# Layer 1 of a hybrid decoder step: keys in the index queries' room, stacked values later in the sample workspace's room, sample search behind the prompt's scores

## The chip, the core and the metric

The kernel runs on one core of one Trainium2 chip. The metric is the device time of one execution in microseconds (us), median of several executions. TensorE (PE) multiplies matrices and transposes, VectorE (DVE), ScalarE (ACT) and GpSimd (POOL) work element by element, and SyncE (SP) and ACT issue most of the transfers. Each engine works through its own list of instructions in order.

## The reference, cut to what matters

One inference step of a two-layer decoder, with a prompt of 1024 tokens and eight sample rows (one new token each, 1024 cached). The change lies in layer 1, whose mixer is a sparse attention: an indexer scores every key for every query, the best 256 keys of each query are kept, and 16 query heads attend to those alone over 4 key/value heads.

```
def dsa_attend(qpos, q, qi, wi, k, v, ki, topk):
    dots = jnp.einsum('bqhd,bkd->bqhk', qi, ki).astype(jnp.float32)
    score = jnp.einsum('bqhk,bqh->bqk', jax.nn.relu(dots), wi.astype(jnp.float32))
    causal = kpos[None, None, :] <= qpos[None, :, None]
    _, idx = lax.top_k(jnp.where(causal, score, -jnp.inf), topk)
    k_sel = gather(k, idx)
    v_sel = gather(v, idx)
    s = jnp.einsum('bqngd,bqknd->bqngk', qg, k_sel).astype(jnp.float32) * (HEAD_DIM ** -0.5)
    p = jax.nn.softmax(jnp.where(valid, s, -jnp.inf), axis=-1).astype(v.dtype)
    o = jnp.einsum('bqngk,bqknd->bqngd', p, v_sel)
...
def dsa_mixer(xn, pos, past_kv, past_idx_k, page_table, w_in, idx_g, idx_b, w_out):
    q, k, v, qi, ki, wi = split_cols(xn @ w_in, C_SIZES)
    if page_table is None:
        o = map_query_blocks(lambda pb, qb, qib, wib: dsa_attend(pb, qb, qib, wib, k, v, ki, topk), pos, q, qi, wi)
    else:
        o = dsa_attend(pos, q, qi, wi, k_all, v_all, ki_all, topk)
    return o @ w_out, (jnp.stack([k, v], axis=2), ki)
```

## The kernel before, in words

Layer 1's mixer takes about the stretch from 1340 to 2000 us of the span. Its parts run side by side:

- **The projection** (dense_cols, L339 to L341 by way of mm3): for each tile of 128 output columns (index queries qi, queries q 0 to 7, keys k 0 and 1, values v 0 and 1, in this order) three chunks of tokens with 24 matmuls each, d<-xh and d<-xl. The weight of each tile is split into a high and a low part (whif on ACT, wlof on DVE). ev_raw copies a finished tile to "raw1", and post_q, post_k or post_v goes on: rotation (rope, a shuffle on DVE and three products on POOL), splits into high and low, and natural-order copies by TensorE transposes (nat_out, "b<-small,raw").
- **Index scores** (idx_scores, L1956 on PE, L229 `sc<-rl` on DVE), for six blocks of 128 queries in groups [2,3], [4,5] and [6,7]; blocks 0 and 1 need no choice.
- **The prompt's search** (top_select): bit by bit, 31 steps for each group, a count of scores above a threshold (L1993 on DVE `tjk<-sc` or `tjk<-top`, or L215 `tjk<-sc` on ACT) and three small operations on 128x2 tiles. It ends in the mask of each block (flags l1.m2 to l1.m7).
- **The sample's search** (gen_dsa_dec): index scores of the cache, then eight steps, each a count over 128x1025 on DVE (L2263 `tjk<-hk`), a matmul with 128x1 output that sums over partitions (L2268 `b<-small,grpc`), and small operations; then ranks (two scans), eight transposes (L251 `b<-small,hk`), one-hot rows (L218 `hk<-tmpd`), and eight matmuls that turn them into a list of rows (L2324 `b<-hk`, "the list" below), which DVE reads (`tmpd<-b`). Later come the gathers of the listed rows and the sample's attention.
- **The prompt's attention** (dsa_units): for each of eight query blocks and four key/value heads a unit of four heads. A score group of TensorE (L530 `s<-ks,q1b`), a masked maximum on DVE (L533), an exponential on ACT, transposes, and the product with the values: blocks 0 to 4 (PLAIN) take the natural values "nat" kept in VF (L2099), blocks 5 to 7 take "stacked" values vs, a high and a low copy side by side (L2103). The queries q1b come by transfers from device memory. The out projection starts when all 32 units and the sample's attention are done.

Four large tiles of one pool matter here, each of the pool's size: hx (index queries of the prompt), hk (the sample's workspace), ks1 (the keys' stacks) and vs1 (the values' stacks); the last two can only be made in room that hx and hk have left.

The order of the program comes from two stages. Generators (streams) yield costs and wait for flags ("need"); a driver lets the one with the least accumulated cost go on. Its list then goes through a scheduler that places instructions by a simulated timeline, so that the order on an engine differs from that of the code. A wait on a flag therefore sets when instructions are written, not a wait on the chip; on the chip an instruction waits for the data and the room that it needs, and for its place in its engine's list.

## Time and profile before

| | us |
|---|---|
| three runs | 2834.07, 2835.79, 2839.3 |
| median | 2835.79 |
| profiled execution | 2833.61 |
| its span | 2831.9 |
| PE busy over the span | 2556.9 (90%) |
| DVE busy over the span | 2230.6 (79%) |
| ACT busy over the span | 1328.7 (47%) |
| POOL busy over the span | 1337.9 (47%) |

The shares of the whole span are averages over stages with different limits. In the stretch of the change they turn round for a while: DVE is busier than PE. Busy PE time is modelled, and a matmul takes longer where the granted clock (PEclk, 1.00 is full speed) is low.

### The profile page before, as it was taken

The page shows a single profiled execution, that of the slowest core. Times are in us where ns is not written, and L with a number is a line of the kernel's source. Part 1 is how long each engine was busy: PE and PEld are TensorE (multiplying, and loading weights), DVE is VectorE, ACT ScalarE, POOL GpSimd, SP SyncE. Part 2 cuts the span into 40 slices and gives each one's busy share as a digit, 9 for nine tenths or more (in the row PEclk, how much of TensorE's full clock was granted, in tenths as well). Part 3 has the DMA queues.
Part 4 walks back from the last instruction along what each step waited for, and adds up shares of the span by engine and source line. Part 5 has one row for each costly group of instructions (what it writes and reads, how often), then busy time and mean ns, then how long its engine had stood idle before and what let it go on. Part 6 is the DMA issues. An engine that isn't in the chain of part 4 may idle for free.

```text
span 2831.9 us, 48456 instructions
## 1 busy us (share of the span) xinstructions
PE 2556.9 (90%) x17916; PEld 2391.4 (84%) x17916; DVE 2230.6 (79%) x4125; ACT 1328.7 (47%) x2726; POOL 1337.9 (47%) x992
## 2 busy tenths in 40 slices
PE   7988889989999899999888758999979999899998
PEld 6977788989999899999777744567979999898998
DVE  4466887787777899986468999998477887899995
ACT  4235766344434433433256457779333343533331
POOL 2376454345555666620544525133135555667630
PEclk9999999999999999999989868999989999999999
DMA  4844567304444634322353325321303444644331
GB/s 132 269 149 142 164 213 251 131 16 139 136 154 135 205 126 143 128 98 93 97 154 106 119 77 129 81 59 31 128 23 109 143 147 145 207 135 131 125 105 61
DMA packets 272095, 363.30 MB, mean 128 GB/s; under 512 B 25184, under 2 KB 200456, under 8 KB 271604
## 3 DMA queue, kind: packets, MB, share of 16 engines
q1 hardware_dynamic: 217124, 290.48, 32.1%
q0 software_dynamic: 15120, 49.81, 5.3%
q10 hardware_dynamic: 39616, 19.93, 2.5%
q8 instruction: 141, 2.31, 0.3%
q14 instruction: 94, 0.77, 0.1%
HBM read 252.19 MB, written 108.00 MB: 127 GB/s over the span
## 4 chain that ended last, share of the span: by engine, by line
PE 47%; DVE 21%; issue 4%; ACT 4%; DMA 3%; POOL 2%; SPq 0%; ACTq 0%; DVEq 0%; POOLq 0%
PE d L1501 10%; PE d L1503 9%; PE d L1502 9%; DVE fdu L218 4%; PE d L339 3%; PE d L341 3%; PE d L340 3%; PE s L530 2%; PE o L2099 2%; PE t L251 2%; DVE xT L218 1%; DVE x1a L218 1%; DVE small L229 1%; DVE fd L218 1%; DVE tjk L1993 1%
## 5 line engine op out<-in xcount | busy, mean ns | idle before, releaser
L1501 PE MATMUL d<-xoph,fs 128*128 128x258 f32 x768 | 221.6, 289 | 19.7 <-ACT z L215 13.0
L221 POOL TENSOR_TENSOR fraw<-fraw,small 128x1024 f32<-128x1024 f32 x64 | 134.4, 2104 | 209.9 <-DMA fraw<-in_ffn_w 181.7
L218 DVE TENSOR_TENSOR xT<-xT,d 128x258 f32<-128x258 f32 (+1 forms) x472 | 185.5, 424 | 44.6 <-PE d L341 26.9
L1502 PE MATMUL d<-xoph,fs 128*128 128x258 f32 x768 | 219.2, 286 | 0.0
L1503 PE MATMUL d<-xoph,fs 128*128 128x258 f32 x768 | 218.4, 285 | 0.0
L339 PE MATMUL d<-xh,whif 128*128 128x344 f32 (+1 forms) x616 | 201.9, 329 | 11.4 <-DVE small L226 5.7
L341 PE MATMUL d<-xh,wlof 128*128 128x344 f32 (+1 forms) x616 | 198.0, 325 | 3.9 <-DVE wlof L218 3.9
L340 PE MATMUL d<-xl,whif 128*128 128x344 f32 (+1 forms) x616 | 200.6, 326 | 0.0
L221 POOL TENSOR_TENSOR z<-z 128x516 f32<-128x516 f32 x112 | 168.8, 1507 | 47.0 <-DMA d_zp<-z 39.2
L215 ACT ACTIVATE s<-s,small 128x128 f32<-128x128 f32 (+7 forms) x192 | 149.7, 782 | 66.8 <-DVE small L533 65.5
L339 PE MATMUL d<-xh,whi 128*128 128x344 f32 x504 | 169.9, 338 | 11.4 <-ACT whi L215 5.9
L341 PE MATMUL d<-xh,wlo 128*128 128x344 f32 x504 | 165.0, 330 | 12.2 <-DVE wlo L218 11.8
L1501 PEld LDWEIGHTS d<-xoph,fs 128*128 128x128 f32 x768 | 147.2, 192 | 23.8 <-ACT z L215 16.3
L340 PE MATMUL d<-xl,whi 128*128 128x344 f32 x504 | 167.2, 332 | 0.0
L218 DVE TENSOR_TENSOR fdu<-fraw,fdu 128x256 fp32r<-128x256 f32 x168 | 165.0, 993 | 0.0
L1501 PE MATMUL d<-zoph,fdu 128*128 128x258 f32 x448 | 129.7, 292 | 26.9 <-DVE xT L218 13.7
L1502 PEld LDWEIGHTS d<-xoph,fs 128*128 128x128 f32 x768 | 147.6, 192 | 0.6 <-DVE xoph L218 0.6
L1503 PEld LDWEIGHTS d<-xoph,fs 128*128 128x128 f32 x768 | 147.7, 192 | 0.0
L1503 PE MATMUL d<-xop,fl 128*128 128x258 f32 x512 | 146.3, 286 | 1.4 <-DVE fl L218 1.4
L1501 PE MATMUL d<-xop,fl 128*128 128x258 f32 x512 | 146.4, 286 | 0.0
L1502 PE MATMUL d<-xop,fl 128*128 128x258 f32 x512 | 146.2, 286 | 0.0
L251 PE MATMUL t<-small,s 128*128 128x128 f32 x864 | 139.4, 280 | 5.7 <-DVE tm L218 3.4
(484 smaller groups left out, 9902.2 us busy)
## 6 DMA issues: line engine op xcount, KB each, us to landing
fraw<-in_ffn_w SPq DMA_DIRECT2D x120, 512.0 KB
zr<-d_zp SPq DMA_DIRECT2D x98, 516.0 KB
d_zp<-z POOLq DMA_DIRECT2D x56, 516.0 KB, 3.2
kp<-in_cache_fox_kv SPq DMA_DIRECT2D x64, 256.0 KB
vp<-in_cache_fox_kv SPq DMA_DIRECT2D x64, 256.0 KB
q1b<-d_q ACTq DMA_DIRECT2D x32, 512.0 KB
d_zp<-z SPq DMA_DIRECT2D x28, 516.0 KB
wraw<-in_ab_w_in SPq DMA_DIRECT2D x21, 512.0 KB
```

The lines of the kernel that those rows point to most:

```text
L215: return nc.scalar.activation(out=out, in_=in_, func=func, **kw)
L218: return nc.vector.tensor_tensor(out=out, in0=a, in1=b, op=op)
L221: return nc.gpsimd.tensor_tensor(out=out, in0=a, in1=b, op=op)
L251: return nc.tensor.transpose(out, in_, ident[:n, :n])
L339: mm(ps, lhsT=wh, rhs=ah, start=(j == 0), stop=False)
L340: mm(ps, lhsT=wh, rhs=al, start=False, stop=False)
L341: i = mm(ps, lhsT=wl, rhs=ah, start=False, stop=(j == last))
L530: mm(p[:, :m], lhsT=lh[x], rhs=ks[:, k0:k0 + m], start=(x == 0), stop=(x == 1 and not dg))
L1501: mm(o, lhsT=wh[:, k], rhs=hi[:, cols], start=(start and k == 0), stop=False, skip_group_check=not start)
L1502: mm(o, lhsT=wh[:, k], rhs=lo[:, cols], start=False, stop=False, skip_group_check=not start)
L1503: i = mm(o, lhsT=wl[:, k], rhs=hi[:, cols], start=False, stop=(k == nk - 1), skip_group_check=not start)
L2099: mm(po[:64], lhsT=VF[g // 2][:, kb, 64 * (g % 2):64 * (g % 2) + 64], rhs=ph, start=(kb == 0), stop=(kb == i))
```

## The change

1. post_k: the keys' stacks wait for the flag hx_free (all index scores written) and no longer for hk_free (the list written).
2. post_v: the natural copies of the values no longer wait for the keys' stacks and hx_free. The stacked values are made afterwards, from the kept copy VF, when hk_free is set, by the same operations (a copy on ACT and a difference on POOL for each of four heads), and set new flags l1.vs0 and l1.vs1.
3. dsa_units: units of blocks 5 to 7 also wait for these two flags.
4. gen_dsa_dec: the eight steps of the sample's search wait for the flag l1.sc6 (the index scores of all groups written).

```
--- before.py
+++ after.py
@@ -1797,7 +1797,7 @@
         def post_k(t, raw):
             yield from rope(raw)
             nc.gpsimd.tensor_copy(out=K1[:, t], in_=raw[:, S:T])
-            yield from need("hk_free")
+            yield from need("hx_free")
             if t == 0:
                 KS[0] = H(F32R, "ks1")
             for e in range(2):
@@ -1808,17 +1808,23 @@
 
         def post_v(t, raw):
             yield 500.0
-            yield from need("l1.k1", "hx_free")
-            if t == 0:
-                VS[0] = H(F32R, "vs1")
             g = nat_out(raw, O["dsa_kv_p"][0, 0, :, 1], t, O["dsa_kv_s"][0, :, 0, 1],
-                        [VS[0][:, 2 * t + e, :S].rearrange("p (i f) -> p i f", i=8) for e in range(2)], flip=False,
                         vn=VN1[:, t * 128:(t + 1) * 128], keep=VF)
             yield next(g)
             yield next(g)
             yield next(g)
             flags.add("l1.v%d" % t)
             yield from g
+            yield from need("hk_free", *["l1.vs0"] * t)
+            if t == 0:
+                VS[0] = H(F32R, "vs1")
+            for e in range(2):
+                v = VS[0][:, 2 * t + e, :S].rearrange("p (i f) -> p i f", i=8)
+                src = VF[t][:, :, e * 64:(e + 1) * 64]
+                act(v[:, :, :64], src)
+                gt(v[:, :, 64:], src, _r(v[:, :, :64]), SUB)
+                yield 2000.0
+            flags.add("l1.vs%d" % t)
 
         kib = []
 
@@ -2136,7 +2142,7 @@
             for z in range(2):
                 q_load(*order[z])
             for z, (i, g) in enumerate(order):
-                yield ("need", ("l1.m%d" % i,))
+                yield ("need", ("l1.m%d" % i,) + (("l1.vs0", "l1.vs1") if i not in PLAIN else ()))
                 if z + 2 < len(order):
                     q_load(*order[z + 2])
                 yield make(i, g)
@@ -2237,6 +2243,7 @@
             mm(p[:, 0:1], lhsT=bm128[:64], rhs=wc[:, 1:2], start=True, stop=True)
             act(scd[:, S:NK], p[:, 0:1])
             yield 1500.0
+            yield from need("l1.sc6")
 
             dig = small("1", [128, 8], "digc", dt=I32)
             dma(out=dig, in_=C["dig"])
```

Every engine has the same instructions as before; they stand in another order. Lines up to L1811 keep their numbers, those behind are six and, from the sample's search on, seven higher in the changed kernel.

**PE, first step of the sample's search.** Before: the matmul of the first step (L2268) stands amid the projection of the first queries, with 32 of 160 score matmuls (L1956) still behind it.

```order
8740 L1956 MATMUL s<-hx 128x384 x2
8741 L339 MATMUL d<-xh_14297,whif 128x344
8742 L340 MATMUL d<-xl_14299,whif 128x344
8743 L341 MATMUL d<-xh_14297,wlof 128x344
8744 L339 MATMUL d<-xh_14297,whif 128x344
8745 L340 MATMUL d<-xl_14299,whif 128x344
8746 L2268 MATMUL b<-small,grpc 128x1
8747 L341 MATMUL d<-xh_14297,wlof 128x344
8748 L339 MATMUL d<-xh_14297,whif 128x344
```

After (L2275 is the same matmul):

```order
8994 L340 MATMUL d<-xl_14299,whif 128x344
8995 L341 MATMUL d<-xh_14297,wlof 128x344
8996 L339 MATMUL d<-xh_14298,whif 128x344
8997 L340 MATMUL d<-xl_14300,whif 128x344
8998 L2275 MATMUL b<-small,grpc 128x1
8999 L341 MATMUL d<-xh_14298,wlof 128x344
9000 L339 MATMUL d<-xh_14298,whif 128x344
```

It now stands behind all score matmuls and 249 projection matmuls later (614 of the layer's 936 stand ahead of it, counted from the first score, where it was 365).

**PE, last steps, list and first attention scores.** Before, the eight steps are spread between projection matmuls, the last stands at 802 of 936, and transposes and list come ahead of the projection's last 72 matmuls:

```order
9253 L339 MATMUL d<-xh_14298,whif 128x344
9254 L340 MATMUL d<-xl_14300,whif 128x344
9255 L341 MATMUL d<-xh_14298,wlof 128x344
9256 L251 MATMUL b<-small,hk 128x128 x8
9257 L2324 MATMUL b<-hk 128x128 x8
9258 L251 MATMUL b<-small,raw_17254 128x128 x8
9259 L251 MATMUL b<-small,raw_17254 8x128
9260 L251 MATMUL b<-small,raw_17407 128x128 x4
9261 L339 MATMUL d<-xh_14297,whif 128x344
9262 L340 MATMUL d<-xl_14299,whif 128x344
9263 L339 MATMUL d<-xh_14297,whif 128x344
```

Behind these follow the rest of the 72 matmuls, transposes, the small matmuls with QX, and the first attention score:

```order
9338 L341 MATMUL d<-xh_14298,wlof 128x344
9339 L251 MATMUL b<-small,raw_17725 128x128 x8
9340 L251 MATMUL b<-small,raw_17725 8x128
9341 L2372 MATMUL b<-small,QX 128x1 x2
9342 L530 MATMUL s<-ks_17461,q1b 128x128 x16
```

After, the last three steps stand in a row behind 864 matmuls, and the 72 follow at once:

```order
9251 L340 MATMUL d<-xl_14300,whif 128x344
9252 L341 MATMUL d<-xh_14298,wlof 128x344
9253 L2275 MATMUL b<-small,grpc 128x1 x3
9254 L251 MATMUL b<-small,raw_17254 128x128 x8
9255 L251 MATMUL b<-small,raw_17254 8x128
9256 L339 MATMUL d<-xh_14297,whif 128x344
9257 L340 MATMUL d<-xl_14299,whif 128x344
9258 L339 MATMUL d<-xh_14297,whif 128x344
```

and the list (L2331) stands behind the 72, three rows ahead of the first attention score:

```order
9328 L251 MATMUL b<-small,hk 128x128 x8
9329 L251 MATMUL b<-small,raw_17387 128x128 x4
9330 L251 MATMUL b<-small,raw_17531 128x128 x4
9331 L251 MATMUL b<-small,raw_17387 128x128 x4
9332 L251 MATMUL b<-small,raw_17531 128x128 x4
9333 L251 MATMUL b<-small,raw_17387 8x128
9334 L251 MATMUL b<-small,raw_17531 8x128
9335 L2331 MATMUL b<-hk 128x128 x8
9336 L251 MATMUL b<-small,raw_17708 128x128 x8
9337 L251 MATMUL b<-small,raw_17708 8x128
9338 L2379 MATMUL b<-small,QX 128x1 x2
9339 L530 MATMUL s<-ks_17400,q1b 128x128 x16
```

What moved: the list went from ahead of the last projection tile to behind it; the attention stands behind the list in both.

**DVE, ahead of the first attention score.** `s,small<-s,mask` is the masked maximum of a score group, `tjk,small<-sc` and `<-top` counts of the prompt's search, `small 128x2` its small operations, `tmpd<-b` the reading of the list. Before, the list was read 49 instructions ahead of this place:

```order
1713 L1993 TENSOR_SCALAR tjk,small<-sc,small 128x768
1714 L226 TENSOR_SCALAR small<-small 128x2
1715 L229 SCALAR_TENSOR_TENSOR small<-small 128x2 x2
1716 L226 TENSOR_SCALAR small<-small 128x2
1717 L1993 TENSOR_SCALAR tjk,small<-sc,small 128x768
1718 L229 SCALAR_TENSOR_TENSOR small<-small 128x2
1719 L1993 TENSOR_SCALAR tjk,small<-top,small 128x1024
1720 L229 SCALAR_TENSOR_TENSOR small<-small 128x2
1721 L226 TENSOR_SCALAR small<-small 128x2
1722 L1993 TENSOR_SCALAR tjk,small<-sc,small 128x768
1723 L229 SCALAR_TENSOR_TENSOR small<-small 128x2
1724 L533 ISA s,small<-s,mask_14902 128x128
```

After:

```order
1725 L218 TENSOR_TENSOR tmpd<-b,bd_17712 128x128
1726 L229 SCALAR_TENSOR_TENSOR small<-small 128x2
1727 L2340 TENSOR_REDUCE tmpd<-tmpd 128x16
1728 L226 TENSOR_SCALAR small<-small 128x2
1729 L226 TENSOR_SCALAR small<-tmpd 128x16 x2
1730 L1999 TENSOR_SCALAR tjk,small<-sc,small 128x768
1731 L1999 TENSOR_SCALAR tjk,small<-top,small 128x1024
1732 L229 SCALAR_TENSOR_TENSOR small<-small 128x2 x2
1733 L226 TENSOR_SCALAR small<-small 128x2
1734 L1999 TENSOR_SCALAR tjk,small<-sc,small 128x768
1735 L229 SCALAR_TENSOR_TENSOR small<-small 128x2
1736 L533 ISA s,small<-s,mask_14902 128x128
```

The list is now read 13 instructions ahead of the first masked maximum. Counted from the first score of the layer, the first masked maximum was DVE instruction 417 and is now 441: twelve more 128x2 operations of the form SCALAR_TENSOR_TENSOR, six of the form TENSOR_SCALAR, four counts 128x768 and two counts 128x1024 stand ahead of it. The last score operation (`sc<-rl`) stands at 132 (146 before), the masks of blocks 2 and 3 at 356 and 373 (384 and 397). Further on, the mask of block 4 stands at 613 (it was 655) with 32 of the layer's 192 masked maxima ahead of it (44 before), and that of block 7, the last, at 909 (930) with 103 ahead of it (110 before).

On POOL only the rotation of the second key tile moved, from behind the clearing of QX to ahead of the second key tile's stacks. On POOL and ACT the operations of the stacked values still stand ahead of the attention's. SP's and ACT's transfers are the same ones.

## Rows read from the trace of the kernel before

Busy times of the windows are in the order PE, PEld (weight loads), DVE, ACT, POOL, each with its count of instructions; then PEclk, DMA share and GB/s. In the groups by shape the numbers are total busy us, mean ns of one | idle us ahead of them and what ended it.

**Rows 1.** Windows of the mixer by stage: stretch, busy us per engine, PEclk, DMA, GB/s.

```profile
1500.00:1687.00 187.00, 129.19 (x726) 123.03 (x724) 172.56 (x372) 100.85 (x231) 86.30 (x47) 0.83 0.33 98
1687.00:1780.00 93.00, 77.26 (x317) 45.47 (x317) 83.99 (x286) 68.41 (x185) 42.86 (x44) 0.82 0.56 142
1780.00:1860.00 80.00, 78.87 (x354) 41.81 (x353) 72.15 (x232) 61.61 (x143) 5.88 (x8) 1.00 0.26 67
1860.00:2000.00 140.00, 132.81 (x753) 104.10 (x752) 118.21 (x298) 123.30 (x258) 57.29 (x61) 1.00 0.17 48
```

**Rows 2.** Chain that ended last, 1490 to 1700: start us, us, what.

```profile
1651.05 4.47 DVE hk L218 x2
...
1657.02 3.76 PE b L2324 x16
...
1682.15 4.28 DMA q1b<-d_q
1686.47 0.70 PE s L530 x2
```

**Rows 3.** Waits, 1560 to 1700: waiting <- waited for: total us, times, longest.

```profile
PEld b L2268 <- DVE small L226: 18.0, 4, 6.2
...
PE b L2324 <- DVE small L229: 13.6, 1, 13.6
...
PE b L251 <- DVE small L229: 9.1, 1, 9.1
```

**Rows 4.** DVE's groups by shape, 1501 to 1687, before the first masked maximum.

```profile
L229 DVE SCALAR_TENSOR_TENSOR small<-small 128x2 int32<-128x2 int32 x44 | 20.5, 469 | 0.2
L226 DVE TENSOR_SCALAR small<-small 128x2 int32<-128x2 int32 x49 | 18.0, 368 | 0.5
L229 DVE SCALAR_TENSOR_TENSOR small<-small 128x2 int32<-128x2 f32 x45 | 16.0, 357 | 9.6 <-ACT tjk L215 9.1
```

**Rows 5.** The same view, 1619 to 1780.

```profile
L1993 DVE TENSOR_SCALAR_CACHE_REDUCE tjk<-top,small 128x1024 bf16<-128x1024 bf16 x15 | 19.1, 1271 | 0.1
L1993 DVE TENSOR_SCALAR_CACHE_REDUCE tjk<-sc,small 128x768 bf16<-128x768 f32 x17 | 17.2, 1010 | 0.3
...
L226 DVE TENSOR_SCALAR small<-small 128x2 int32<-128x2 int32 x49 | 8.6, 183 | 0.6
L229 DVE SCALAR_TENSOR_TENSOR small<-small 128x2 int32<-128x2 int32 x44 | 8.1, 187 | 0.3
L229 DVE SCALAR_TENSOR_TENSOR small<-small 128x2 int32<-128x2 f32 x44 | 7.7, 177 | 2.4 <-ACT tjk L215 1.6
```

**Rows 6.** Timeline 1604 to 1609: start us, us, instruction.

```profile
1605.44 2.42 POOL L221 TENSOR_TENSOR r1l<-raw,r1h 128x1032 fp32r<-128x1032 f32 x1 [4.89 <-ACT r1h L215]
...
1605.55 2.33 DVE L229 SCALAR_TENSOR_TENSOR small<-small 128x2 int32<-128x2 int32 x1
```

**Rows 7.** Timeline: the second search step's count on DVE and its matmul on PE.

```profile
1523.34 1.28 DVE L2263 TENSOR_SCALAR_CACHE_REDUCE tjk<-hk,small 128x1025 bf16<-128x1025 f32 x1
...
1543.70 0.28 PE L2268 MATMUL b<-small,grpc 128*128 128x1 f32 x2
```

**Rows 8.** Windows of 20 us around the attention's start, columns as in rows 1.

```profile
1640.00:1660.00 20.00, 4.92 (x22) 4.58 (x23) 19.62 (x47) 9.64 (x27) 8.21 (x4) 0.50 0.08 27
1660.00:1680.00 20.00, 16.75 (x108) 15.83 (x107) 19.38 (x45) 11.79 (x25) 7.55 (x5) 0.95 0.27 80
1680.00:1700.00 20.00, 12.08 (x48) 9.20 (x48) 16.20 (x66) 16.95 (x47) 2.79 (x3) 0.56 0.59 164
1700.00:1720.00 20.00, 15.73 (x57) 8.82 (x58) 18.77 (x78) 16.59 (x50) 7.65 (x9) 0.76 0.57 131
1720.00:1740.00 20.00, 16.17 (x66) 9.16 (x67) 16.63 (x61) 14.79 (x38) 13.63 (x16) 0.83 0.58 148
```

**Rows 9.** Timeline: the last mask on DVE, the out projection's first matmul on PE.

```profile
1880.25 0.42 DVE L226 TENSOR_SCALAR sc<-tjk 128x1024 bf16<-128x1024 bf16 x1
...
1997.32 0.36 PE L339 MATMUL d<-xh,whif 128*128 128x344 f32 x1
```

19 lines of the change are left out of this document (13 added, 6 removed).

## The prediction

> **What bounds the kernel now.** I read the windows by stage first, since the shares of the whole span mix stages with different limits. From 1500 to 1687 us, where projection, the two searches and the last rotations run side by side, DVE is busy 172.56 of 187.00 us (92%) and PE 129.19 (69%) [rows 1]. From 1687 to 1780, when the attention has begun beside the prompt's search, DVE still leads with 90%, PE has 83% at a granted clock of 0.82. From 1780 to 1860 PE has 78.87 of 80.00 us, and from 1860 to 2000 132.81 of 140.00: there PE is the limit. So a delay or gain before 1780 is one of DVE's list, and what of it is left at 1780 meets a full PE.
>
> The chain says the same in its pieces: one-hot rows on DVE at 1651.05, the list on PE at 1657.02, further counts and masks on DVE (left out there), the transfer of q1b at 1682.15, the first attention score at 1686.47 [rows 2]. The waits give PE's side: it waits 18.0 us in all for the small operations of four search steps, 13.6 for the list's one-hot rows and 9.1 for the ranks' transposes [rows 3]. That is PE's time while DVE is the limit, so the waits are room and not loss as long as DVE doesn't wait for what PE then has late. DVE's own idle time before 1687 is 187.00 - 172.56 = 14.4 us, of which 9.1 end with a count on ACT [rows 1, 4].
>
> **The change part by part.** No instruction is removed or added on any engine; the price is one of places.
>
> *The search behind the scores.* Each of its eight counts, scans and small operations stays on DVE between the first score and the first attention score. The order shows what came ahead of them: DVE had 417 instructions ahead of the first masked maximum and has 441. The 24 more are the prompt's search, which no longer shares its early stretch with the sample's. At the quiet stretch's durations they cost 4 counts x 1.010 = 4.0, 2 x 1.271 = 2.5, 12 x 0.18 = 2.2 and 6 x 0.183 = 1.1, together 9.8 us [rows 5]. In the crowded stretch the small ones cost 0.41 (between 0.469 and 0.357) and 0.368 [rows 4], which makes 4.9 and 2.2 of them and 13.6 in all. I take the quiet price, 9.8, since the added counts stand in the last part, near the list, where the rotations on POOL are over. On a path where DVE is 92% busy all of it counts: **the first masked maximum comes at about 1687 + 10 = 1697.**
>
> Why a small operation has two prices is in the timeline: one of 128x2 that started at 1605.55 took 2.33 us, just as a POOL difference of 2.42 us had started at 1605.44 [rows 6]; the mean in the quiet stretch is 0.187. The Trainium skill, "SBUF — State Buffer", section "Who interferes with whom", says that the two engines share a port pair, and that a VectorE instruction with two SBUF inputs waits out a GpSimd instruction that reads SBUF; the trace agrees with 2.33 beside 2.42. By that rule the price of a moved operation depends on whether a POOL difference runs at its new place, and the sum would be 9.8 or 13.6 as above.
>
> This lengthening is the largest thing that the trace of before doesn't fix for the new order. Over the crowded stretch it is 44 x (469 - 187) + 49 x (368 - 183) + 45 x (357 - 177) ns = 12.4 + 9.1 + 8.1 = 29.6 us [rows 4, 5]. POOL's instructions are the same, so I leave it unchanged; it may shift by a quarter either way, 7 us, because other DVE instructions now meet them.
>
> *PE's search matmuls.* Before, the second step's count started at 1523.34 and its matmul, queued behind projection and scores, came at 1543.70 [rows 7]: 20 us in which the sample's search stood still and DVE did the prompt's instead. After, the steps stand where PE reaches them; the last three in a row. PE then waits for DVE once more, and behind it in PE's queue stand the last projection tile's 72 matmuls: 72 x 16.75 / 108 = 11.2 us at the mean of the 20 us in which before ran them [rows 8]. They are hidden, since PE has 187.00 - 129.19 = 57.8 us free there [rows 1], and the list now comes behind them instead of ahead. If that cover were gone they would cost their 11.2.
>
> *Keys and values.* The stacks' room was the reason for the old waits. But the attention's first score stands behind the list's matmuls in PE's order before and after, so keys that are ready earlier start nothing earlier: cost and gain nil. On POOL the second key tile's rotation passes the clearing of QX and of the keys' stacks, all ahead of the attention; nil. The stacked values' operations on ACT and POOL stand ahead of the attention's first ones as before, and the first unit that needs them is the 21st of 32; the new waits of blocks 5 to 7 are nil. Below nothing there is no room either, as nothing waited for vs. Transfers on SP and ACT's queue are the same; the q1b transfer of 4.28 us ends just ahead of the first score [rows 2] and stays behind the same search masks, which the order has 24 to 28 instructions earlier on DVE. At most a part of the 4.28 us comes back, inside the range.
>
> *What is given back.* After the first masked maximum the prompt's search has 24 instructions fewer to do, so DVE's part of the 9.8 us returns until the last mask, which stands 21 instructions earlier in the order than before. At that point 103 of 192 masked maxima are done instead of 110. The last 82 of before took from 1880.25 to the out projection's first matmul at 1997.32, 1.43 us each [rows 9]; seven more are 10.0 us of PE work. Against it stands the earlier mask: 21 instructions, of which 14 are the seven maxima with their readouts and the rest small ones, some 5 to 8 us. That leaves +2 to +5. Counted by PE instead: a lag of 5 to 8 us at 1780 into a stretch with 1.1 + 7.2 = 8.3 us of idle PE time until 2000 [rows 1] keeps between 0 and 8. **I take +4**, the middle of both, with ends 0 and +10 (nothing given back).
>
> **Sum.** 2833.6 (the profiled execution) + 4 = 2837.6. The median of the three runs lies 2.2 above the profiled execution, so by it the sum is 2839.8; I set the forecast near the lower, at 2838.
>
> **The rivals.**
>
> *Faster by less crowding.* The search's steps no longer stand between scores and rotations, the scores end 14 DVE instructions earlier and the projection reaches its rotations with four stops fewer, so POOL runs its differences earlier and beside fewer small operations. If half of the 29.6 us of lengthening and half of the 14.4 us of idle time went, that is 22.0 against 9.8, and the attention starts 12 earlier: 2833.6 - 12 = about 2822. For it: PE's 18.0 us of waits in the steps [rows 3]. Against it: ACT's counts (9.1 us of DVE's idle time) and POOL's work are the same. It decides from 15.5 us of relief on, which gives -5.7.
>
> *Slower by a cold PE.* The last 72 matmuls no longer stand between list and attention. In before PE was busy 4.92 of 20 us from 1640 to 1660 at a granted clock of 0.50 (the lower of its two levels, 1.2 GHz), and the 72 brought 0.95 from 1660 to 1680; even so the attention began at 0.56, 0.76 and 0.83 [rows 8]. Now the waiting for ranks and list, 13.6 + 9.1 us [rows 3], stands right ahead of the attention. PE's 43.98 us of work from 1680 to 1740 at a mean clock of 0.72 would be 63 us at 0.50, over the 60 that DVE leaves it: 3 us, and with the whole lag of 10 kept and some DVE waiting for scores 15 in all, **about 2848**. It decides once PE takes longer than DVE for a unit before 1740. The Trainium skill, "TensorE: Matmul & The Clock Gate", section "HAM oscillation — how this bites in real kernels", speaks against this change: work in bursts with idle gaps between them starts each burst at half clock. The trace agrees with 0.50 after the gap at 1640.
>
> *The change doesn't do what it says.* If keys and values start nothing, and DVE's order is only shuffled, the time stays: 2834 to 2836. For it: the attention stands behind the list on PE in both orders. Against it: 24 instructions did move.
>
> **How the numbers follow.** About 0.2%, 5.7 us, is what a measurement of this kernel can tell from no change: 2830.1 to 2841.5. My forecast has 0.42, of which 0.32 fall inside that band and 0.10 above; no effect has 0.12, all inside; faster by less crowding 0.24, of which 0.01 inside; the cold PE 0.22, all above. That gives faster 0.23, same 0.45, slower 0.32. The range reaches to both rivals' times and leaves out the ends of each: 2822 to 2849.
>
> **What would show it.** Right: first masked maximum at 1692 to 1702; DVE's busy share from 1500 to there still above 90%; the lag shrinking to 0 to 5 us by the last mask and PE over 95% busy from 1780 on; the 72 matmuls done ahead of the ranks' transposes. Wrong toward faster: the 128x2 operations at a mean well below 0.36 us, first masked maximum before 1685. Wrong toward slower: a granted clock at 0.5 for the first 40 us of the attention, and DVE waiting for scores there. The forecast falls too if some wait far off, such as for the sample's gathers ahead of the out projection, ends last.

## The result, and the profile after

The changed kernel is slower: 2851.73 us in the median of four runs (2850.44 to 2852.15) against 2835.62 for the kernel before beside them, ratio 1.0054 with a 95% interval of 1.0037 to 1.0071. Measured again beside other kernels (below) the ratio was 1.0034 (1.0021 to 1.0047), so by the two ratios the loss is some 10 to 15 us. The profiled execution took 2851.57 us, its span is 2849.3.

Times from here on are best counted from the layer's first score operation, because executions differ ahead of it whatever the kernel. These are its rows in the timelines of before and after, start and duration in us:

```profile
1382.92 0.42 DVE L226 TENSOR_SCALAR sc<-rl,small 128x384 f32<-128x384 f32 x1 [9.96 <-ACT rl L215]
```

```profile
1388.13 0.42 DVE L226 TENSOR_SCALAR sc<-rl,small 128x384 f32<-128x384 f32 x1 [9.96 <-ACT rl L215]
```

All instructions ahead of this place stand in the same order in both kernels, yet the second is 5.2 us later. In the 19 profiles of this study the place lies between 1378.5 and 1391.6, with the same code ahead of it, so these 5.2 us belong to the execution. The layer's stretch from the first score to the out projection repeats within 1 us: 614.4 and 614.2 us in two executions of the kernel before, 624.5 and 625.2 in two of the changed one. What follows it differs by up to 3.4 us between two executions of one kernel.

Timeline of the kernel after: the list read by DVE, the first masked maximum, the last mask, the last masked maximum, and the out projection's first matmul (the last mask and the projection answer to [rows 9]).

```profile
1698.76 0.28 DVE L218 TENSOR_TENSOR tmpd<-b,bd 128x128 f32<-128x128 f32 x1
...
1705.69 0.29 DVE L533 CUSTOM_DVE_ANT_0 s<-s,mask 128x128 f32<-128x128 f32 x1
...
1884.34 0.42 DVE L226 TENSOR_SCALAR sc<-tjk 128x1024 bf16<-128x1024 bf16 x1
...
2000.99 0.74 DVE L533 CUSTOM_DVE_ANT_0 s<-s,sc,small 128x512 f32<-128x512 f32 x1
...
2012.62 0.32 PE L339 MATMUL d<-xh,whif 128*128 128x344 f32 x1
```

The same places of the kernel before, as far as they are not in [rows 9]:

```profile
1660.80 0.29 DVE L218 TENSOR_TENSOR tmpd<-b,bd 128x128 f32<-128x128 f32 x1 [0.16 <-PE b L2324]
...
1687.20 0.29 DVE L533 CUSTOM_DVE_ANT_0 s<-s,mask 128x128 f32<-128x128 f32 x1 [1.29 <-PE s L530]
...
1986.02 0.74 DVE L533 CUSTOM_DVE_ANT_0 s<-s,sc,small 128x512 f32<-128x512 f32 x1
```

Counted from the first score, the list is read at 310.6 instead of 277.9, the first masked maximum comes at 317.6 instead of 304.3 (+13.3), the last one at 612.9 instead of 603.1 (+9.8), the out projection at 624.5 instead of 614.4 (+10.1). The distance from the list to the first masked maximum fell from 26.4 to 6.9 us; whether the one waits for the other is asked below.

The windows from the first score to the first masked maximum, from there to the last mask, and from the mask to the out projection, first before, then after (columns as in [rows 1]):

```profile
1382.92:1687.20 304.28, 227.80 (x1278) 212.71 (x1278) 239.71 (x473) 160.09 (x370) 141.55 (x80) 0.86 0.39 112
1687.20:1880.25 193.05, 174.08 (x757) 98.45 (x757) 176.31 (x557) 142.54 (x353) 56.88 (x57) 0.92 0.40 102
1880.25:1997.32 117.07, 111.99 (x649) 90.05 (x647) 96.13 (x256) 109.83 (x229) 48.32 (x55) 1.00 0.14 41
```

```profile
1388.13:1705.69 317.56, 235.55 (x1278) 219.74 (x1278) 249.85 (x503) 165.06 (x382) 144.55 (x81) 0.84 0.37 108
1705.69:1884.34 178.65, 161.53 (x697) 91.04 (x697) 160.12 (x507) 127.13 (x322) 47.61 (x52) 0.92 0.41 105
1884.34:2012.62 128.28, 122.73 (x707) 98.45 (x707) 103.90 (x278) 118.72 (x249) 51.95 (x59) 1.00 0.15 45
```

Ahead of the first masked maximum DVE has 10.1 us more to do (249.85 instead of 239.71) and stands idle 3.1 us longer (67.7 instead of 64.6). From there to the last mask it has 16.2 us less to do and stands idle 1.8 longer. So the last mask comes 1.1 us earlier than before, at 496.2 from the first score instead of 497.3. But 89 masked maxima are left behind it where 82 were, at 1.44 us each (1.43 before), and that stretch is 11.2 us longer. The layer's +10.1 is -1.1 + 11.2.

A finer cut of the attention: the windows from the first masked maximum to the first of block 4 (the 65th), to the first of block 6 (the 129th) and to the last, first before, then after:

```profile
1687.20:1813.97 126.77, 110.33 (x474) 64.05 (x474) 115.32 (x377) 97.17 (x257) 45.16 (x48) 0.87 0.49 121
1813.97:1900.19 86.22, 81.86 (x390) 48.85 (x388) 77.74 (x231) 64.14 (x138) 20.40 (x20) 1.00 0.22 62
1900.19:1986.02 85.83, 83.40 (x483) 67.64 (x482) 72.35 (x192) 80.92 (x167) 35.22 (x40) 1.00 0.11 32
```

```profile
1705.69:1832.20 126.51, 109.68 (x475) 64.04 (x474) 111.20 (x362) 94.18 (x251) 43.31 (x47) 0.88 0.49 123
1832.20:1913.15 80.95, 79.91 (x388) 48.73 (x386) 72.75 (x217) 59.09 (x130) 16.66 (x19) 1.00 0.22 60
1913.15:2000.99 87.84, 83.94 (x485) 68.46 (x484) 73.03 (x193) 82.40 (x171) 35.19 (x41) 1.00 0.12 34
```

The whole stretch took 298.8 us before and 295.3 after. DVE had 265.4 us to do in it and has 257.0, 8.4 less; only 3.5 of them came back. In the first window DVE has 4.1 us less to do and stands idle 3.9 longer, so nothing comes back there, though PE has 16.8 us free in it. The lag of 13.3 us is still 13.1 at the first maximum of block 4, 7.7 at that of block 6 and 9.8 at the end. PE was busy 275.6 and is busy 273.5, nearly all of the time once block 4 has begun. The clock, aligned in this way, is the same (0.87 and 0.88 in the first window).

Ahead of the first masked maximum the waits of PE in the kernel after, 1560 to 1720 us (these answer to [rows 3]):

```profile
PE b L2275 <- DVE small L226: 25.9, 6, 5.9
...
PE b L251 <- DVE small L229: 12.4, 1, 12.4
...
PE s L530 <- DMA q1b<-d_q: 6.7, 3, 5.3
...
PE b L2331 <- DVE hk L218: 4.2, 1, 4.2
```

and those of DVE from 1505 to 1705.6, of which the first was 9.1 us before [rows 4] and the next two were not over 0.5:

```profile
DVE small L229 <- ACT tjk L215: 11.5, 10, 1.9
DVE sc L229 <- ACT rl L215: 2.1, 3, 1.0
DVE shf L1767 <- ACT raw L215: 1.1, 2, 0.9
...
DVE small L226 <- PE b L2275: 0.2, 1, 0.2
```

The last line is all that DVE waits there for the sample's chain on PE.

DVE's groups by shape in that stretch (the 128x2 rows answer to [rows 4]):

```profile
L226 DVE TENSOR_SCALAR small<-small 128x2 int32<-128x2 int32 x55 | 24.8, 456 | 0.6
L229 DVE SCALAR_TENSOR_TENSOR small<-small 128x2 int32<-128x2 f32 x51 | 18.9, 373 | 11.9 <-ACT tjk L215 11.5
L218 DVE TENSOR_TENSOR wlof<-wrawf,whif 128x1024 fp32r<-128x1024 f32 x7 | 16.3, 2323 | 0.0
...
L229 DVE SCALAR_TENSOR_TENSOR small<-small 128x2 int32<-128x2 int32 x50 | 13.5, 275 | 0.5
```

### The profile page after: what moved, and what is told of

The parts are those of the page before. It is cut to its first block, busy times and chain, and to the rows that moved or that the text cites. A ratio compares the mean times of both kernels' runs of the same rounds, so it can differ in the third digit from the quotient of the medians.

```text
span 2849.3 us, 48472 instructions
## 1 busy us (share of the span) xinstructions
PE 2564.5 (90%) x17916; PEld 2400.3 (84%) x17916; DVE 2227.9 (78%) x4125; ACT 1327.8 (47%) x2726; POOL 1335.6 (47%) x992
## 4 chain that ended last, share of the span: by engine, by line
PE 46%; DVE 18%; issue 6%; ACT 4%; DMA 4%; POOL 2%; SPq 0%; DVEq 0%; POOLq 0%; ACTq 0%
PE d L1501 10%; PE d L1503 10%; PE d L1502 10%; DVE fdu L218 4%; PE d L340 3%; PE d L341 3%; PE d L339 3%; PE s L530 2%; PE t L251 2%; PE o L2105 2%; PE o L2109 1%; DVE x1a L218 1%; DVE xT L218 1%; ACT tjk L215 1%; DVE tjk L1999 1%
## 5 line engine op out<-in xcount | busy, mean ns | idle before, releaser
L341 PE MATMUL d<-xh,wlo 128*128 128x344 f32 x504 | 165.8, 332 | 11.9 <-DVE wlo L218 11.7
L215 ACT ACTIVATE tjk<-sc,small 128x384 bf16<-128x384 f32 (+3 forms) x124 | 99.4, 801 | 96.9 <-DVE small L226 75.4
```

The costliest lines, as they stand in the source:

```text
L215: return nc.scalar.activation(out=out, in_=in_, func=func, **kw)
L341: i = mm(ps, lhsT=wl, rhs=ah, start=False, stop=(j == last))
```

## The experiments

All ratios are to the kernel before run beside it on the same chip, with the 95% interval. Places are in us from the first score, read from the starts in each kernel's timeline.

| kernel | ratio | list read | first masked maximum | last |
|---|---|---|---|---|
| before | | 277.9 | 304.3 | 603.1 |
| before_again | 1.0011 (0.9997 to 1.0025) | 278.3 | 304.6 | 602.9 |
| changed | 1.0054 (1.0037 to 1.0071) | 310.6 | 317.6 | 612.9 |
| changed_again | 1.0034 (1.0021 to 1.0047) | 310.6 | 317.5 | 613.6 |
| search_early | 1.0028 (1.0017 to 1.0039) | 270.0 | 304.7 | 616.9 |
| search_late_alone | 1.0021 (1.0005 to 1.0038) | 310.5 | 321.7 | 616.6 |
| keys_early_alone | 1.0029 (1.0010 to 1.0048) | 271.4 | 307.1 | 612.4 |
| values_late_alone | 0.9999 (0.9985 to 1.0014) | 277.9 | 304.2 | 603.3 |
| prompt_search_later_a | 1.0015 (1.0000 to 1.0030) | 273.6 | 286.8 | 616.0 |
| prompt_search_later_b | 0.9990 (0.9975 to 1.0004) | 261.5 | 297.8 | 608.3 |
| before_prompt_search_later_b | 1.0021 (1.0011 to 1.0032) | 270.6 | 299.3 | 611.8 |
| before_prompt_search_later_c | 1.0013 (1.0002 to 1.0024) | 271.0 | 298.3 | 605.6 |
| ten_counts_early | 0.9993 (0.9981 to 1.0006) | 278.6 | 306.2 | 606.5 |
| ten_counts_late | 1.0007 (0.9996 to 1.0018) | 278.5 | 304.8 | 609.1 |
| changed_ten_counts_late | 1.0060 (1.0034 to 1.0087) | 311.1 | 318.0 | 629.6 |
| changed_prompt_search_later_d | 1.0031 (1.0015 to 1.0047) | 309.3 | 314.2 | 619.5 |
| changed_prompt_search_later_e | 1.0021 (1.0004 to 1.0039) | 307.4 | 313.0 | 614.1 |
| changed_list_behind_4 | 1.0004 (0.9986 to 1.0022) | 341.5 | 298.6 | 608.0 |
| changed_list_behind_2 | 1.0023 (1.0008 to 1.0038) | 334.9 | 298.5 | 607.4 |

The kernel before against itself gave 1.0011, so a ratio says little under 0.0015; the places in the layer, which repeat within 1 us, tell the kernels apart.

### The parts of the change

The search put back, keys and values as changed:

```
             act(scd[:, S:NK], p[:, 0:1])
             yield 1500.0
-            yield from need("l1.sc6")
```

> The changed kernel with one part undone: the sample's search no longer waits for the prompt's scores (l1.sc6); keys and stacked values stay as changed. In its order the first masked maximum is DVE instruction 412 counted from the first score (417 before, 441 changed). Theory 'place in DVE's list': the first masked maximum comes at 1683 to 1690 and the time is 2832 to 2838, as before, so the search's wait is the whole loss. Rival 'keys and values' (their new waits cost, for instance through later stacks): the time stays at 2845 to 2852 though the search is early.

Half met: the first masked maximum is where it was before (304.7), but the end is 13.8 us later than before and the ratio 1.0028. So the search's wait is not the whole loss. (The times forecast are set against some 2835 us; the kernel before took 2844.89 beside this one.)

The other way round, the wait alone added to the kernel before:

> The kernel before with the search's wait alone added; keys and values as before. First masked maximum at DVE instruction 451. Theory 'place in DVE's list': 10 instructions more ahead than in the changed kernel, so the first masked maximum is 1 to 6 us later than its 1705.7 and the time is 2850 to 2858. Rival 'keys and values': the loss is smaller than in the changed kernel, 2836 to 2845.

First masked maximum 4.1 us later than in the changed kernel, as the ten instructions said, and last maximum at 616.6, 13.5 later than before. Its ratio, 1.0021, came out lower than expected. This kernel writes the sample rows' new keys and values wrongly, and the record doesn't show why; its row tells the effect of an order of work and is not that of a usable kernel.

The two halves of the rest, each alone in the kernel before:

```
         def post_k(t, raw):
...
-            yield from need("hk_free")
+            yield from need("hx_free")
```

> The kernel before with one part of the change: the keys' stacks wait for the end of the index scores instead of the list; stacked values and search as before. Theory 'keys early let the sample's gathers and the attention meet': the loss of search_early (ratio 1.0028) is here too, 1.002 to 1.004, with TensorE waiting some 5 us each for the sample's gathered keys and on ACT's list between 1720 and 1760. Rival 'values late': the loss is in the later stacks of the values, so this kernel is at 1.000 within 0.1%.

> The kernel before with the other part: stacked values made after the list from the kept natural copies, with the new waits of blocks 5 to 7; keys and search as before. Its order on DVE and PE up to the last mask has the marks of the kernel before (first masked maximum at 417, last mask at 930). Theory 'keys early': ratio 1.000 within 0.1%. Rival 'values late': 1.002 to 1.004.

The later stacked values cost nothing (last maximum at 603.3), as my prediction had it. The early keys alone cost 9.3 us. Their first masked maximum is 2.8 us late; the rest is lost between the first maximum of block 1 (322.7, before 325.4) and that of block 4 (440.1, before 431.0). DVE's waits in this kernel from 1685.5 to 1818.5:

```profile
DVE s L533 <- PE s L530: 3.7, 1, 3.7
DVE s L533 <- PE o L2099: 3.5, 2, 2.6
```

In the kernel before the same two come to 1.6 and 1.3 in that stretch. The order on DVE there has seven masked maxima fewer ahead of block 6's mask (97 instead of 104), so part of it is more search work ahead of the same maxima. From the first maximum of block 1 to that of block 4 the stretch is 11.7 us longer: DVE has 7.2 us more to do and stands idle 4.5 longer, so the work is the larger part. Why TensorE is late in those two places I did not settle: the gathered-keys part of the expectation is not borne out, as TensorE waited 1.3 us for the gathered keys and not 5.

Both once more, beside one another:

> The changed kernel once more, beside the kernel before and the two kernels of this call on the same chip, so that the parts can be set against the whole. If the change's loss is that of its parts added (search behind the scores +5.7, keys and values +6.2, as measured apart), the ratio is about 1.004; if the parts overlap, about 1.003; the first measurement gave 1.0054.

> The kernel before against itself, with a second profile. Every theory: ratio 1.000 within 0.1%. Its profile tells how much of the 5.2 us by which the changed kernel was already late at the layer's first score belongs to the execution and not to the change: all instructions ahead of that place stand in the same order in both, so I expect the last masked maximum of the first layer at 530 to 540 here too, and the layer's stretch from the first score to the out projection at 614 us within 3.

The layer of before_again took 614.2 us, as expected. The ratio of changed_again, 1.0034, stands between the two forecasts, 1.003 and 1.004, and its interval holds both; the places have to tell. Early keys cost 9.3 us alone, the late search 13.5, both with late values 9.8 to 10.7: the parts are not added. With the search late, the early keys give 4 us back (317.6 instead of 321.7 at the first masked maximum).

### Is it the place of the prompt's steps in DVE's list?

My first theory was the one of the prediction's sum, without its last term: the 24 instructions ahead of the first masked maximum set the loss and a full TensorE keeps it. Two kernels with the planner's costs changed, so that the prompt's steps come later (both with the early keys):

```
-CE = {2: 1.5, 4: 2, 6: 3}
+CE = {2: 2.5, 4: 4, 6: 6}
```

> As search_early, with one thing more: the prompt's bit search is given larger costs in the planner (early costs 2.5, 4 and 6 for the three groups instead of 1.5, 2 and 3), so fewer of its steps stand ahead of the attention. First masked maximum at DVE instruction 343, 74 instructions and, at the shortest durations, 24.6 us of DVE work earlier than before. Theory 'place in DVE's list, kept by a full PE': first masked maximum at about 1655 to 1670, and 60 to 100% of that shift is kept to the end, time 2812 to 2824. Rival 'given back' (the term of my sum by which most of a shift at the attention's start returns by the last mask): first masked maximum as early, but the time 2830 to 2836, since the masks then come later. Rival 'cold PE': a colder start eats the gain, clock at 0.5 for the first 40 us of the attention.

> As search_early, with the prompt's early costs 2, 6 and 9: first masked maximum at DVE instruction 375, 15.2 us of DVE work earlier than before, masks 2 and 3 still ahead of it. Theory 'place in DVE's list, kept by a full PE': first masked maximum at 1668 to 1678, time 2820 to 2829. Rival 'given back': time 2831 to 2836.

The first masked maximum came 17.5 and 6.5 us earlier, and neither kernel was faster: the stretch from there to the last maximum grew to 329 and 310 us. The theory "kept by a full PE" fell for shifts to the early side. In prompt_search_later_a the mask of block 4 was written at 438.6 and the first maximum that needs it came at 440.2: the masks had become the limit.

> The kernel before, keys, values and sample's search as before, with the planner's early costs of the prompt's search at 2, 6 and 9 (the costs of prompt_search_later_b, which had the keys early too and came out at 0.999). First masked maximum at DVE instruction 375. Theory 'every loss is DVE's idle time': without the 9 us that the early keys cost, 0.995 to 0.998, a kernel faster than both. Rival 'the early keys cost nothing once the search is later': 0.998 to 1.001.

> As before_prompt_search_later_b with late costs 2, 3 and 3 as well (2, 2.5 and 2.5 before): first masked maximum at 364, last mask at 921 with 107 maxima ahead of it, nearer to the kernel before (930, 110) than the other (957, 120). Theory: 0.995 to 0.999. Rival 'masks too late': over 1.000, with masked maxima waiting for masks.

The same without the early keys: again earlier starts (299.3 and 298.3) and later ends. Neither ratio is in the range that the theory gave (0.995 to 0.998 and 0.995 to 0.999). For the second, "masks too late" has the number right (1.0013), but the mask of block 4 was there at 421.0 and its first maximum came at 440.7. No version faster than the kernel before came of it.

Ten useless counts added on DVE, ahead of the first masked maximum and late in the search:

```
                 ts(cd, F, 1 << b, None, ALU.bitwise_xor)
+                if grp[0] == 6 and b == 26:
+                    padc = small("1", [128, 1], "padc")
+                    for _ in range(10):
+                        nc.vector.tensor_scalar(out=jk[:, 1, :768], in0=jk[:, 1, :768], scalar1=0.0, scalar2=None,
+                                                op0=ALU.is_ge, op1=ADD, accum_out=padc)
```

> The kernel before with ten useless counts of 128x768 added on DVE (1.00 us each by the traces, 10.0 in all, results unused) right ahead of the first masked maximum, in the chain of the prompt's search of blocks 6 and 7. Theory 'DVE's list is the limit up to the last masked maximum': its work there is 10 us more, nothing takes it back, last masked maximum 8 to 11 us later counted from the first score (603 in the kernel before), ratio 1.0028 to 1.004. Theory of my prediction 'given back against a PE with some idle time': 0 to 8 us of it are left. Rival 'hidden': 0.

> The same ten counts at the search's sixth-last bit, some 150 us later, where my prediction took TensorE for the limit (78.87 of 80.00 us busy). Theory 'DVE's list is the limit up to the last masked maximum': 8 to 11 us here too. Theory of my prediction 'TensorE is the limit from 1780 on': DVE has 8 of 80 us free there, so 0 to 4 us.

The early ones moved the last masked maximum by 3.4 us, the late ones (b == 5) by 6.0, and neither ratio is clear of 1. The early ones don't measure what they should: the planner put other steps of the prompt's search behind the attention's start in their place, and the first masked maximum moved by 1.9 us, not by 10. What they do show is that DVE is not the only limit: 10 us of work more is 3 to 6 us of time.

### Is TensorE the floor of the attention's stretch?

The late counts in the changed kernel, where DVE has 8.4 us less to do behind the first masked maximum:

> The changed kernel with the ten useless counts (10.0 us of DVE work) of ten_counts_late at the same bit of the prompt's search; first masked maximum and masks of blocks 4 and 5 keep their places in the order (441, 613, 654). Theory 'TensorE is the floor from the first masked maximum on': DVE has 257 us of work in that stretch against 265 in the kernel before, so the ten counts find more room than the 6.0 us that they cost there: 0 to 3 us, last masked maximum at 613 to 616 from the first score. Rival 'DVE's waits for ACT hold the stretch': they cost what they cost before, 6 us or more, 619 or later.

The last masked maximum came at 629.6, 16.7 us later, but this doesn't answer the question. The lag is there before the first of the counts runs: the first maximum of block 2, at the same place in DVE's list, is already 9.6 us late and that of block 3 12.8. The waits point to another order on other engines. DVE's timeline in that stretch:

```profile
1748.81 0.17 DVE L229 SCALAR_TENSOR_TENSOR small<-small 128x2 int32<-128x2 f32 x1
1755.49 0.75 DVE L2404 CUSTOM_DVE_ANT_0 Pd<-ka,bneg,small 128x512 f32<-128x512 f32 x1 [6.51 <-remote]
```

and POOL's wait there (1722 to 1788):

```profile
POOL kpg L2375 <- ACT xh L215: 10.0, 1, 10.0
```

POOL issues the sample's gathers (kpg) in one list with the attention's last products (xl). Here one xl that waited for ACT stood ahead of the gathers for 10.0 us, where the changed kernel has 2.2; the gathered keys came late, and DVE stood 6.5 us before the sample's scores Pd with the prompt's work behind them. From block 3 on, where the counts stand, the lag grew by 3.9 us. Whether TensorE alone is the floor stays open; that it is busy 273.5 of 295.3 us is what the windows show.

### What holds the first masked maximum

With the late search left as it is, the prompt's steps moved back behind the attention's start by the planner's costs:

```
-CM = {2: 2, 4: 2.5, 6: 2.5}
-CE = {2: 1.5, 4: 2, 6: 3}
+CM = {2: 2, 4: 2.2, 6: 2.2}
+CE = {2: 1.5, 4: 3, 6: 4.5}
```

> The changed kernel with the planner's early costs of the prompt's search at 1.5, 3 and 4.5 and late ones at 2, 2.2 and 2.2: search behind the scores and keys as changed, but the first masked maximum back at DVE instruction 419 and the last mask at 934 with 112 maxima ahead of it (before 417 and 930 with 110, changed 441 and 909 with 103). Theory 'place of the prompt's steps': first masked maximum at 304 to 310 us from the first score, last at 603 to 608, ratio 1.000 to 1.002. Rival 'the late search itself' (its steps meet more waits for ACT's counts and scores): first masked maximum at 312 or later, ratio 1.003 or more.

> The same with early costs 1.5, 2.5 and 3.5 alone: first masked maximum at 428, last mask at 918 with 106 maxima ahead, half way. Theory 'place of the prompt's steps': first masked maximum at 309 to 314, last at 606 to 610, ratio 1.001 to 1.003. Rival: as the changed kernel, 317 and 613.

For the first of them the rival's forecast is the one that came (314.2, where it said 312 or later, and 1.0031); the second lies between (313.0 as the theory said, the last at 614.1 as the rival). In the first 22 of the 24 instructions are taken away from ahead of the first masked maximum, and it comes 3.4 us earlier instead of 13. Its timeline there:

```profile
1695.95 0.29 DVE L218 TENSOR_TENSOR tmpd<-b,bd 128x128 f32<-128x128 f32 x1
...
1700.90 0.29 DVE L533 CUSTOM_DVE_ANT_0 s<-s,mask 128x128 f32<-128x128 f32 x1
```

The list is read at 309.3 from the first score, hardly earlier than in the changed kernel (310.6), and the first masked maximum follows 4.9 us behind it. From the first score to the first masked maximum DVE had 6.8 us less to do than in the changed kernel (243.04 instead of 249.85) and stood idle 3.5 longer, among others 14.9 us for ACT's counts (11.5 in the changed kernel):

```profile
1386.66:1700.90 314.24, 232.67 (x1278) 216.80 (x1278) 243.04 (x474) 158.86 (x369) 140.63 (x80) 0.85 0.37 109
```

```profile
DVE small L229 <- ACT tjk L215: 14.9, 10, 3.3
```

The list's place near the first masked maximum led me to a second theory: the attention's first scores stand behind the list's matmuls in TensorE's order, so the sample's chain from its first step to the list gates the attention. To part it from "DVE's waits", the list was moved behind the attention's start, with the late search kept:

```
             tt(rank[:, :S], rank[:, :S], eq[:, :S], MUL)
             yield 26000
+            yield from need("l1.u4")
...
                 yield make(i, g)
+                if z == 4:
+                    flags.add("l1.u4")
```

> The changed kernel with one wait more: the ranks' transposes and the list of the sample's search wait until five units of the prompt's attention are written, so that the attention stands ahead of the list on TensorE and DVE. First masked maximum at DVE instruction 394 (changed 441, before 417), list read at 532, last mask at 934 with 112 maxima ahead. Theory 'the list gates the attention': first masked maximum at 290 to 303 us from the first score, 15 us or more earlier than in the changed kernel, list read 40 us or more later than its 310.6; last masked maximum 600 to 611. Rival 'DVE's waits beside the late search': first masked maximum at 308 or later.

> The same with three units: first masked maximum at DVE instruction 394, list read at 508, last mask at 957 with 120 maxima ahead. Theory and rival as for changed_list_behind_4; last masked maximum within 4 us of it.

The forecast of the theory came: the first masked maximum is at 298.6 and 298.5, 19 us earlier than in the changed kernel and 5.7 earlier than before, with the search as late as the change put it and the list read at 341.5 and 334.9. The last masked maximum came at 608.0 and 607.4, 5 us earlier than in the changed kernel, and the first of the two kernels is not told from the kernel before.

But the two kernels don't show that the attention waited for the list, since the work on DVE accounts for the same 19 us. With the list 47 DVE instructions went from ahead of the first masked maximum to behind it (394 instead of 441), 17 of the sample's work and 30 of the prompt's search. The window of changed_list_behind_4 from the first score to the first masked maximum:

```profile
1391.60:1690.23 298.63, 230.77 (x1258) 214.67 (x1259) 231.51 (x447) 154.17 (x352) 141.49 (x76) 0.85 0.40 116
```

DVE has 18.3 us less to do than in the changed kernel (231.51 instead of 249.85) and stands idle 67.1 us instead of 67.7. The 18.9 us are DVE's work; a wait that had ended would show in the idle time. The trace of the changed kernel says the same from the other side. DVE waited 0.2 us for the sample's chain on PE, and PE, done with what stands behind the list at 1699.6, waited not for the list but for the queries q1b. ACT issues them, in both kernels right behind the start of a count of the prompt's search that waited for DVE's small operations. Before, then after, ACT's and PE's rows:

```profile
1682.07 0.83 ACT L215 ACTIVATE tjk<-sc,small 128x640 bf16<-128x640 f32 x1 [0.46 <-DVE small L226]
1682.15 1.31 ACTq L2055 DMA_DIRECT2D q1b<-d_q  x2
...
1686.47 1.75 PE L530 MATMUL s<-ks,q1b 128*128 128x128 f32 x7 [3.60 <-DMA q1b<-d_q]
```

```profile
1700.58 0.83 ACT L215 ACTIVATE tjk<-sc,small 128x640 bf16<-128x640 f32 x1 [1.00 <-DVE small L226]
1700.66 1.31 ACTq L2061 DMA_DIRECT2D q1b<-d_q  x2
...
1704.96 1.97 PE L530 MATMUL s<-ks,q1b 128*128 128x128 f32 x8 [5.34 <-DMA q1b<-d_q]
```

From the issue to the first score it is 4.3 us in both, so all 13.3 us of lag are there at the issue. In the 19 profiles the first masked maximum lies between 286.8 and 321.7 us from the first score, DVE's work ahead of it between 217.1 and 253.0, and the difference, DVE's idle time, between 63 and 75. So the first masked maximum goes with the work that DVE's list has ahead of it; the list's place counts by what the planner puts ahead of it on DVE. No kernel here holds that work fixed and moves the list alone.

The rest of changed_list_behind_4, from its first masked maximum to the first of block 4:

```profile
1690.23:1827.54 137.31, 115.89 (x494) 66.41 (x494) 126.82 (x401) 101.87 (x268) 49.35 (x51) 0.87 0.43 110
```

From the first to the last masked maximum it takes 309.4 us: what was moved came behind the start as DVE work, 126.82 of 137.31 us in this window. That is the other side of the balance that all these kernels show.

## Why the prediction was wrong

**The direction.** I forecast 2838, no change that can be measured, in a range of 2822 to 2849. The measured 2851.73 is above it and the kernel is slower. Of the 17.4 us between the spans of the two profiled executions 5.2 lie ahead of the layer and 2.2 behind it, no more than executions of one kernel differ there, and 10.1 in the layer. Those 10.1, put on the profiled 2833.6, would be 2843.7: above the forecast, inside the range, at the upper end, +10, of my term. Beside changed_again the medians differ by 10.6 us.

**The step that failed** is "What is given back", the price of the earlier mask: "21 instructions, of which 14 are the seven maxima with their readouts and the rest small ones, some 5 to 8 us". It counts DVE's work and takes DVE's idle time as unchanged, without a reason. Up to the last mask DVE's work fell by 6.0 us (416.0 to 410.0), as priced. But DVE stood idle 4.9 us longer (81.3 to 86.2), 3.1 ahead of the first masked maximum and 1.8 behind it, so the mask came 1.1 us earlier and not 5 to 8. In the second profiles of both kernels it is 7.4 us less work, 7.6 more idle time and a mask 0.2 later. The other side of the term held: seven more maxima behind the mask cost 11.2 us (I had 10.0). With "+2 to +5" for -1.1 + 11.2 the sum was 5 to 8 us short, and the middle between it and the count by PE, "between 0 and 8", did not mend that. The waits that grew are in the traces: ahead of the first masked maximum DVE's for ACT's counts (9.1 to 11.5 us) and for ACT's `rl` and `raw` (2.1 and 1.1, not over 0.5 before), and between the first masked maximum and the last mask that for the transfers of `rv`, before and after:

```profile
DVE tm L218 <- DMA rv<-d_ls: 3.8, 3, 1.8
```

```profile
DVE tm L218 <- DMA rv<-d_ls: 5.9, 5, 1.4
```

Why these waits grew stays open: no run here changes one of them alone.

**The signs** that I had named for being right came nearly all: the first masked maximum 13.3 us later from the first score, which on the 1687.2 of before is 1700.5, DVE busy 91% from 1505 to it, a lag of no more than 5 us at the last mask, PE 97% busy from block 4 on. A mask on time is no sign of a layer on time when more maxima stand behind it.

**PE's search matmuls** as hidden: right as far as the trace shows, since DVE waited 0.2 us for them. **q1b** is misread: I had it behind the masks, which do come 15.7 and 11.6 us earlier (blocks 2 and 3), but it is issued behind a count, 13.3 us later.

**The 24 instructions** were priced well. Every DVE instruction from the 92nd on at the shortest duration of its form gives some 8.7 us more ahead of the first masked maximum (I had 9.8), lengthening adds 1.5, and the busy time is 10.1 higher. The 3.1 us of idle time make it 13.3.

**The lengthening** was left unchanged in the sum, and that held: the small operations' part was 29.6 and is 50 x (275 - 187) + 55 x (456 - 183) + 51 x (373 - 177) ns = 4.4 + 15.0 + 10.0 = 29.4 us. Other forms changed places: seven weight splits wlof took 2323 ns each instead of the 1403 of this group of the kernel before,

```profile
L218 DVE TENSOR_TENSOR wlof<-wrawf,whif 128x1024 fp32r<-128x1024 f32 x7 | 9.8, 1403 | 0.0
```

6.5 us more, and other instructions were lengthened less.

**Waits of blocks 5 to 7 and stacked values** at nil: right (values_late_alone 603.3). **Early keys** at nil: wrong alone (+9.3), about -4 together with the late search. Here I had argued from the first score alone and not from what follows it, and the four come from a kernel whose sample keys and values are wrong.

**The rivals.** The cold PE gave 2848, nearest to the measurement, and is not the cause. Windows of 20 us from the first masked maximum on (they answer to [rows 8]), before and after:

```profile
1686.00:1706.00 20.00, 15.91 (x54) 10.75 (x54) 16.32 (x71) 16.78 (x50) 3.24 (x3) 0.50 0.59 163
1706.00:1726.00 20.00, 13.58 (x61) 8.57 (x60) 17.78 (x71) 15.87 (x47) 11.40 (x13) 0.84 0.60 129
1726.00:1746.00 20.00, 18.58 (x72) 9.48 (x72) 17.25 (x58) 15.78 (x40) 14.07 (x16) 0.90 0.57 153
```

```profile
1704.50:1724.50 20.00, 15.47 (x56) 11.11 (x56) 15.89 (x69) 15.00 (x47) 3.40 (x4) 0.59 0.58 164
1724.50:1744.50 20.00, 12.96 (x49) 7.14 (x48) 16.47 (x63) 14.15 (x42) 8.92 (x10) 0.76 0.51 110
1744.50:1764.50 20.00, 19.02 (x77) 11.03 (x78) 18.99 (x63) 14.30 (x37) 14.63 (x16) 0.88 0.62 160
```

The clock at the start is 0.59, 0.76 and 0.88 where it was 0.50, 0.84 and 0.90. The attention starts on a cold PE in both, and its stretch became shorter and not longer. In absolute windows one would have read 0.66 from 1700 to 1750 against 0.84 and believed the rival. "Faster by less crowding" failed by its own number: 29.4 against 29.6 us. "Doesn't do what it says" fell with the 10.1 us of DVE work that did move.

## What to carry to other kernels

An order list gives the price of work, not of waiting. Here the work that moved was priced within 2 us, ahead of the first masked maximum and up to the last mask; the 4.9 us by which DVE's idle time grew (7.6 in the second pair of profiles) were in no term. So write idle time into the sum as a term of its own, with a reason if it is left unchanged. Count what stands behind a milestone, too: the last mask came as early as before, and seven more maxima behind it made the loss.

Before an instruction is said to wait for the result that stands ahead of it in an engine's list, look at which of its waits ends last. Here the attention stood behind the list on TensorE and waited for a transfer that ACT issued behind a count. And an experiment that moves a result and, with it, 47 other instructions parts two theories only if their forecasts differ for the other instructions as well.

## What the runs showed of the hardware

- A DVE product of 128x1024 (wlof) took 1403 ns in the mean in the one order and 2323 in the other, by what else ran beside it; the Trainium skill, "SBUF — State Buffer", section "Who interferes with whom", has the rule that a VectorE instruction with two SBUF inputs contends with a GpSimd instruction that reads SBUF. Which instruction is hit changed with the order, the sum hardly did (small operations 29.6 and 29.4 us). That the GpSimd products caused this pair of means was not tried.
- The first transfer of q1b at the attention's start let its first score start 4.3 us after its issue in both kernels (1682.15 to 1686.47, 1700.66 to 1704.96).
- The same code ahead of the layer ended between 1378.5 and 1391.6 us in 19 executions, while the 600 us behind it repeated within 1 us in two executions of each of two kernels. A single profile of a kernel of this length carries some 10 us that are not its own.
